# Two output-weight quarters stored as split halves and loaded again later; one V load and the kept stores queued behind the first Q copies

## The chip, the cores and the metric

One core of a Trainium2 chip runs the whole program. The metric is the device time of one execution in microseconds (us), the median over several runs. TensorE (PE in the profile) multiplies matrices, VectorE (DVE), ScalarE (ACT) and GpSimd (POOL) do the elementwise work, and SyncE (SP) issues most of the DMA transfers between the core's buffers and DRAM. ScalarE can issue transfers too, on a queue of its own.

## The reference

The input x has 2048 rows of 1024 float32. Two layers follow each other, then a last RMS normalisation:

```python
# layer A: chunked gMLP
u, v, z = split(rms_norm(x) @ w_in)                  # 3 x 2048 columns
v = layer_norm(gelu(v)); mixed = W_s (masked) applied over 128-row groups, per head
x = x + (gelu(u) * mixed * silu(z)) @ w_out
# layer B: band attention, 16 heads of 64
k, v = split(rms_norm(x, g_kv) @ w_kv)
q, z = split(rms_norm(x, b_g) @ w_qz)
o = softmax(q k^T / 8 + bias[rel]) v                 # own chunk of 64 rows and the 8 before
x = x + (o * silu(z)) @ wb_out                       # wb_out: 1024 x 1024
out = rms_norm(x, final_g)
```

Everything is float32, and so are the results.

## The kernel before

**Splitting.** Every float32 operand of a large product is split into a high half and a low half (a rounded copy by ScalarE, and the rest by a VectorE subtraction); a product is then three matmuls: high by high, high by low, low by high. The helper `mm3` does that (lines 111 to 113), and `split_in` (lines 241 and 242) splits a weight tile that has arrived as raw float32 in a buffer `raw_...`. Split weights lie in the tag "T", which has eight buffers of 512 KB; the raw ones in two buffers "wr" or four buffers "raw".

**Output product.** `o @ wb_out` is done in Strassen's way with seven products in place of eight, in the order `PHS = (1, 7, 2, 6, 5, 4, 3)`. Products 1, 2 and 3 need a plain quarter of `wb_out` (`o_raw = {1: (0, 0), 2: (1, 0), 3: (1, 1)}`); "quarter 2" below means the quarter of product 2, and so on. Products 4 to 7 need sums of quarters. Each quarter comes in two column parts, q = 0 and 1, and each part is 512 KB for the high half and 512 KB for the low half. The sums are formed once, in tile 1 (`o_sums`), split, and stored as halves in DRAM (`ows`); every later use loads two halves (line 294 or 1787). Quarters 1, 2 and 3 are loaded raw and split again at each use.

**Attention stage.** The 2048 rows are four tiles t of 512 rows. For each tile the kernel walks over eight pairs p of heads, and for each pair over eight steps u (two heads times four blocks of 128 queries). A step computes scores (`score`: matmuls at line 1541, bias and row minimum by VectorE at 1549, exponential by ScalarE at 1559, scaling by GpSimd at 1563), and turns the probabilities of two steps earlier (`flip`: TensorE transposes into `tp` at line 1579, ScalarE copy at 1583, VectorE subtraction at 1584). `value` multiplies by V (line 1604). Between these, TensorE is filled with projections for the next pair (`project`, `gate`: tiles `pj`) and with the output product of the tile before (`outs[t - 1]`), in shares fixed by the table `SHARE`. So products of tile 2 run within tile 3, and tile 3's own output product (`last_all`) begins in the last pair of tile 3 and ends the kernel. There `last_right` fetches the weights; for product 3 they go into the buffer of the transposed probabilities, for product 2 into the four raw buffers.

**Projections and Q.** `project` makes Q for one pair and copies each half to the other 64 partitions with a DMA (line 1482), four copies for a pair: a score needs both places. During the first pair (`held` is set) the stores of K and of the scaled projection weights are put on a list `kept` and issued by `keep_all()` after `values(0, 0)`, which loads V (line 1509).

**Order.** The program text gives a priority, and a planner orders each engine's and each queue's instructions by a simulated time; buffers are assigned in that order too. Where the text wants a fixed order it adds an edge without a semaphore: `follow(ins, names)` puts an instruction behind named ones, and `on_beat(ins)` puts it behind the latest transposes of `flip`. SP's queue issues strictly in order: an issue that waits for its data or its buffer holds all behind it.

Of the kernel before, what the change touches and what calls it, by code (L numbers as in the profile page):

```python
# [33 lines left out]
def trunk_kernel(  # L34
# [30 lines left out]
    }  # L65
    ows = {
        (ph, q): dram.tile([P, 2, 1024], F32, name=f"ows{ph}_{q}")
        for ph in range(4, 8) for q in range(2)
    }
    khd = [  # L70
        [dram.tile([2, P, T], F32, name=f"khd{t}_{p}") for p in range(NPAIR)]
# [134 lines left out]
    def on_beat(ins):  # L206
        if beat:
            tc.add_manual_dep(
                ins.ins, beat[-1],
                mybir.DependencyInfo(mybir.DependencyClass.NoSync, mybir.DependencyReason.DATA),  # L210
                reason="order",
            )
        return ins
# [31 lines left out]
    kept = []  # L245
    held = [0]

    def keep_all():
        while kept:
            nc.sync.dma_start(*kept.pop(0))  # L250

    early_w = {}

# [24 lines left out]
    def o_right(t):  # L278
        def right(ph):
            if (t, ph) in o_early:  # L280
                return o_early.pop((t, ph))
            out = []
            for q in range(2):
                name = f"bo{t}_{ph}_{q}"
                w = [w_tile(f"w{i}_{name}") for i in "hl"]
                if ph in o_raw:
                    raw = raw_w(1, f"raw_{name}")
                    nc.sync.dma_start(raw[:], wb_out[o_raw[ph]][q])
                    hi = split_in(raw, *w)
                    if (ph, q) == (1, 1):  # L290
                        on_beat(hi)
                else:
                    for i in range(2):
                        nc.sync.dma_start(w[i][:].bitcast(F32), ows[ph, q][:, i, :])
                out.append(w)
            return out
        return right
# [1135 lines left out]
    with ExitStack() as bctx:  # L1433
# [22 lines left out]
        def one(t, p, c):  # L1456
# [9 lines left out]
                    yield None  # L1466
            yield acc

        def project(t, p):
            for acc in one(t, p, 1):  # L1470
                yield
            for hd in range(2):
                qh = sb.tile([P, T], F32R, tag="Q", name=f"Qh{t}_{p}_{hd}", bufs=8)
                ql = sb.tile([P, T], F32R, tag="Q", name=f"Ql{t}_{p}_{hd}", bufs=8)
                r, r2 = halves(hd)
                nc.scalar.mul(qh[r, :], acc[r, :], 0.125)
                nc.vector.scalar_tensor_tensor(
                    ql[r, :], acc[r, :], 0.125, qh[r, :].bitcast(F32),
                    op0=ALU.mult, op1=ALU.subtract,
                )  # L1480
                for x_ in (qh, ql):
                    nc.sync.dma_start(x_[r2, :].bitcast(F32), x_[r, :].bitcast(F32))
                qt[t, p, hd] = (qh, ql)
            for acc in one(t, p, 0):
                yield
            for hd in range(2):
                r, r2 = halves(hd)
                kx = sb.tile([P, 2 * T], F32R, tag="K", name=f"K{t}_{p}_{hd}", bufs=4)
                nc.scalar.copy(kx[r, T:], acc[r, :])
                nc.vector.tensor_tensor(  # L1490
                    kx[r2, T:], acc[r, :], kx[r, T:].bitcast(F32), op=ALU.subtract
                )
                if t + 1 < NT:
                    k_store = (khd[t][p][hd], kx[:, T:].bitcast(F32))
                    if held:
                        kept.append(k_store)
                    else:
                        nc.sync.dma_start(*k_store)
                if t > 0:
                    nc.sync.dma_start(kx[:, :T].bitcast(F32), khd[t - 1][p][hd])  # L1500
                kt[t, p, hd] = kx
            if not held:
                keep_all()

        def values(t, p):
            v = vtl[t, p] = sb.tile([P, 8, 256], F32R, tag="V", name=f"V{t}_{p}", bufs=2)
            for i, tt in enumerate((t - 1, t)):
                if tt >= 0:
                    nc.sync.dma_start(v[:, i * TB : (i + 1) * TB, :].bitcast(F32), vhd[tt][:, p])

        def gate(t, p):
            for acc in one(t, p, 2):
# [142 lines left out]
            young.clear()  # L1655

        owed_out = []

        def send(dst, src):
            if la:  # L1660
# [4 lines left out]
        def send_all():  # L1665
            while owed_out:
                on_beat(nc.sync.dma_start(*owed_out.pop(0)))
# [96 lines left out]
        def last_right(ph, q):  # L1764
            name = f"bo_{ph}_{q}"
            if ph == 5:
                v = sb.tile([P, 8, 256], F32R, tag="V", name=f"w{name}", bufs=2)
                w = [v[:, i * 4 : i * 4 + 4, :].rearrange("p a b -> p (a b)") for i in range(2)]
            elif ph == 3:
                if q == 0:  # L1770
                    lw["pt"] = sb.tile([P, 5376], F32R, tag="PT", name=f"w{name}", bufs=1)
                w = [lw["pt"][:, (2 * q + i) * 1024 : (2 * q + i + 1) * 1024] for i in range(2)]
            elif ph == 2:
                w = [
                    sh.tile([P, 1024], F32R, tag="raw", name=f"w{i}{name}", bufs=4)[:]
                    for i in "hl"
                ]
            else:
                w = [w_tile(f"w{i}{name}")[:] for i in "hl"]
            if ph in o_raw:  # L1780
                raw = raw_w(NT - 1, f"raw_{name}")
                nc.sync.dma_start(raw[:], wb_out[o_raw[ph]][q])
                nc.scalar.copy(w[0], raw[:])
                tv(w[1], raw[:], w[0].bitcast(F32), op=sub)
            else:
                for i in range(2):
                    nc.sync.dma_start(w[i].bitcast(F32), ows[ph, q][:, i, :])
            lw[ph, q] = w
# [249 lines left out]
            score(0, 0, u)  # L2038
        held.clear()
        values(0, 0)  # L2040
        keep_all()
        before = None
        for t in range(NT):
            for p in range(NPAIR):
# [14 lines left out]
                for u in range(8):  # L2059
                    if u < 6:  # L2060
                        score(t, p, u + 2)
                    elif p + 1 < NPAIR or t + 1 < NT:
                        score(t + (p + 1) // NPAIR, (p + 1) % NPAIR, u - 6)
                    upto = total * (2 * u + 1) // per
                    take(gen, upto - done)
                    done = max(done, upto)
                    if u == 4:
                        value(t, p, 0)
                    elif u == 0 and before:
                        value(*before, 1)  # L2070
                    flip(t, p, u)
                    drain_all()
                    send_all()
                    square_all()
                    if u and finals:
                        finals.pop(0)()
                    if todo:
                        todo.pop(0)()
                    upto = total * (2 * u + 2) // per
                    take(gen, upto - done)  # L2080
                    done = max(done, upto)
# [64 lines left out]
```

## Time and profile before

| | |
|---|---|
| median of 3 runs | 2639.57 us (2638.92 to 2641.89) |
| profiled execution, its own time | 2640.17 us |
| its span | 2638.1 us |
| TensorE busy | 2604.5 us (99%) |
| VectorE, ScalarE, GpSimd busy | 71%, 50%, 34% |
| DMA, the SP queue | 704.25 MB, 78.1% of the 16 DMA engines |
| DMA in all | 720.31 MB, mean 273 GB/s |

The profile is of one execution. The span runs from its first to its last record; the profiled execution's own time is that of the device, 2.1 us more. Busy times are the union of the instructions of an engine. A wait "X <- Y" says that X's engine stood idle before X, and that Y ended that. A fence of times has the start in us, the duration in us, the engine, the line, the operation, output and inputs, and how many neighbouring instructions were merged; idle time ahead of it stands in brackets. SPq and ACTq are the issues of transfers on those engines' queues; their short durations are the issue alone, and the transfer lands later.

### The profile page before, as it was taken

How to read it: one execution, taken by the hardware profiler on the slowest of the kernel's cores; microseconds unless marked ns; L12 is line 12 of the kernel's file. 1: busy time of each engine (PE TensorE's matmuls, PEld its weight loads, DVE VectorE, ACT ScalarE, POOL GpSimd, SP SyncE). 2: the span in 40 equal slices, each digit the busy share in tenths (PEclk: the TensorE clock that was granted, in tenths of full speed). 3: DMA queues.
4: the chain of work that ended last, by engine and by line, in shares of the span. 5: the costliest groups of instructions: out<-in, count | busy, mean ns of one | idle time of the engine just before them, and what ended most of it. 6: DMA issues, size and time to landing. Idle time of an engine off the chain costs nothing. (4 is left out here: it accounts for less than half of the span.)

```text
span 2638.1 us, 38018 instructions
## 1 busy us (share of the span) xinstructions
PE 2604.5 (99%) x12976; PEld 2177.8 (83%) x12976; DVE 1871.4 (71%) x2942; ACT 1314.7 (50%) x2331; POOL 890.1 (34%) x871
## 2 busy tenths in 40 slices
PE   9999999999999999999999999999999999999997
PEld 7888888788888888888888878888888888888886
DVE  6655676766667668757776767778778777877677
ACT  6422243443433434343466466666656655666564
POOL 4611335143252332203334334343333322332245
PEclk9999999999999999999999999999999999999999
DMA  7898998999988968968886587778787767775676
GB/s 299 316 345 332 347 364 319 315 327 328 333 302 303 331 224 310 342 205 262 322 279 234 184 277 236 233 244 260 248 278 253 228 208 222 252 228 162 192 229 249
DMA packets 275153, 720.31 MB, mean 273 GB/s; under 512 B 28944, under 2 KB 68880, under 8 KB 274960
## 3 DMA queue, kind: packets, MB, share of 16 engines
q1 hardware_dynamic: 268096, 704.25, 78.1%
q10 hardware_dynamic: 6864, 13.63, 1.4%
q8 instruction: 104, 1.70, 0.3%
q14 instruction: 89, 0.73, 0.1%
HBM read 532.69 MB, written 174.59 MB: 268 GB/s over the span
## 5 line engine op out<-in xcount | busy, mean ns | idle before, releaser
L111 PE MATMUL P<-T,S 128*128 128x512 f32 x1248 | 495.3, 397 | 0.0
L113 PE MATMUL P<-T,S 128*128 128x512 f32 x1248 | 487.6, 391 | 0.1
L112 PE MATMUL P<-T,S 128*128 128x512 f32 x1248 | 487.0, 390 | 0.0
L1563 POOL TENSOR_SCALAR pr<-pr,sl 128x640 f32<-128x640 f32 (+4 forms) x256 | 207.9, 812 | 554.1 <-DVE sl L1562 477.7
L111 PE MATMUL pj<-hh_b,wh_b 128*128 128x512 f32 x768 | 318.6, 415 | 0.0
L113 PE MATMUL pj<-hh_b,wl_b 128*128 128x512 f32 x768 | 304.0, 396 | 0.3 <-DVE wl_b L242 0.2
L112 PE MATMUL pj<-hl_b,wh_b 128*128 128x512 f32 x768 | 302.7, 394 | 0.0
L1559 ACT ACTIVATE pr<-pr,nm 128x640 f32<-128x640 f32 (+4 forms) x256 | 195.6, 764 | 198.8 <-DVE nm L1549 196.6
L113 PEld LDWEIGHTS P<-T,S 128*128 128x128 f32 x1248 | 234.3, 188 | 51.0 <-DVE S L463 0.4
L112 PEld LDWEIGHTS P<-T,S 128*128 128x128 f32 x1248 | 235.0, 188 | 44.7 <-DVE T L463 0.4
L111 PEld LDWEIGHTS P<-T,S 128*128 128x128 f32 x1248 | 234.7, 188 | 44.5 <-issue 0.2
L1584 DVE TENSOR_TENSOR pt<-tp,pt 128x640 fp32r<-128x640 f32 (+4 forms) x256 | 188.7, 737 | 48.9 <-ACT pt L1583 46.0
L1549 DVE CUSTOM_DVE_ANT_0 pr<-s,bias 128x640 f32<-128x640 f32 (+4 forms) x256 | 188.3, 736 | 43.8 <-PE s L1541 38.8
L1583 ACT CAST pt<-tp 128x640 fp32r<-128x640 f32 (+4 forms) x256 | 158.6, 619 | 38.5 <-PE tp L1579 32.6
L1579 PE MATMUL tp<-ident,pr 128*128 128x128 f32 x1120 | 166.5, 274 | 8.5 <-DVE pt L1584 7.4
L113 PEld LDWEIGHTS pj<-hh_b,wl_b 128*128 128x128 f32 x768 | 144.2, 188 | 34.5 <-DVE wl_b L242 2.3
L1579 PEld LDWEIGHTS tp<-ident,pr 128*128 128x128 f32 x1120 | 130.9, 140 | 42.5 <-issue 13.8
L111 PEld LDWEIGHTS pj<-hh_b,wh_b 128*128 128x128 f32 x768 | 145.1, 189 | 17.7 <-ACT wh_b L241 1.2
L1604 PEld LDWEIGHTS pv<-pt,V 128*128 128x128 f32 x896 | 142.8, 188 | 20.3 <-DVE pt L1584 3.4
L112 PEld LDWEIGHTS pj<-hl_b,wh_b 128*128 128x128 f32 x768 | 145.1, 189 | 16.5
L1604 PE MATMUL pv<-pt,V 128*128 128x256 f32 (+3 forms) x896 | 154.8, 320 | 0.8 <-ACT pt L1583 0.5
L242 DVE TENSOR_TENSOR wl_b<-raw_b,wh_b 128x1024 fp32r<-128x1024 f32 x96 | 121.0, 1261 | 25.1 <-ACT wh_b L241 22.9
(307 smaller groups left out, 5720.8 us busy)
## 6 DMA issues: line engine op xcount, KB each, us to landing
S<-hsd SPq DMA_DIRECT2D x288, 512.0 KB, 5.3
rw<-in_w_a SPq DMA_DIRECT2D x108, 512.0 KB, 6.2
raw_b<-wk SPq DMA_DIRECT2D x75, 512.0 KB, 4.5
A<-ytd SPq DMA_DIRECT2D x72, 512.0 KB, 5.7
hsd<-S SPq DMA_DIRECT2D x56, 512.0 KB, 4.9
V<-vhd SPq DMA_DIRECT2D x56, 512.0 KB, 5.6
bias<-reld SPq DMA_DIRECT2D x64, 320.0 KB, 4.0
va<-vd SPq DMA_DIRECT2D x32, 512.0 KB, 5.7
```

Source lines behind the costliest of these rows:

```text
L111: first = mm(ps, lh, rh, start=first, stop=False)
L112: mm(ps, lh, rl, start=False, stop=False)
L113: mm(ps, ll, rh, start=False, stop=last)
L242: tv(wl[:], raw[:], wh[:].bitcast(F32), op=sub)
L1549: peak = nc.vector.tensor_tensor_reduce(out=pr[:, c0:].rearrange("p (a b) -> p a b", a=nseg), in0=ps[:, :nseg, :w], in1=bias[:, c0:].rearr ...
L1559: nc.scalar.activation(pr[:, c0:], pr[:, c0:], AF.Exp, scale=-1.0, bias=nm[:], accum_out=sl[:])
L1563: nc.gpsimd.tensor_scalar(pr[:, c0:], pr[:, c0:], sl[:], 1.0, op0=ALU.mult, op1=ALU.mult)
L1579: ins = tpose(tp[:, b, :], pr[:, b * P : (b + 1) * P], ident[:])
L1583: nc.scalar.copy(oh, tp[:, b0:5, :].rearrange("p a b -> p (a b)"))
L1584: nc.vector.tensor_tensor(pt[:, 2560 + o + b0 * P : 2560 + o + 640], tp[:, b0:5, :].rearrange("p a b -> p (a b)"), oh.bitcast(F32), op=ALU ...
L1604: mm(po[:, q0 * P : q1 * P], vtl[t, p][:, i, hs], rhs, start=(i == blocks[0] and j == 0), stop=(i == 7 and j == 1),)
```

## The change

Part one concerns the output weights. `ows` gets entries for products 2 and 3 too. When tile 1's product 3 and tile 2's product 2 have split their raw quarters, the four halves of each are put on a list `halves_out`, and at each later step u, after `flip` and its followers, one of them is stored by ScalarE's queue. Tile 2's product 3 and the last tile's products 2 and 3 then load halves and do not split. Quarter 1 is split at every use as before, and so are quarter 2 in tiles 0 to 2 and quarter 3 in tiles 0 and 1.

Part two concerns the first pair of the attention stage. The names of its four Q copies are collected in `twins`; the V loads of tile 0 and the kept stores that are issued after `values(0, 0)` get an edge that puts them behind those copies on SP's queue.

```diff
     ows = {
         (ph, q): dram.tile([P, 2, 1024], F32, name=f"ows{ph}_{q}")
-        for ph in range(4, 8) for q in range(2)
+        for ph in range(2, 8) for q in range(2)
     }
...
-    def keep_all():
+    def keep_all(names=()):
         while kept:
-            nc.sync.dma_start(*kept.pop(0))
+            follow(nc.sync.dma_start(*kept.pop(0)), names)
...
-                if ph in o_raw:
+                if ph in o_raw and (t, ph) != (2, 3):
                     raw = raw_w(1, f"raw_{name}")
                     nc.sync.dma_start(raw[:], wb_out[o_raw[ph]][q])
                     hi = split_in(raw, *w)
                     if (ph, q) == (1, 1):
                         on_beat(hi)
+                    if (t, ph) in ((1, 3), (2, 2)):
+                        halves_out.extend(
+                            (ows[ph, q][:, i, :], w[i][:].bitcast(F32)) for i in range(2)
+                        )
                 else:
...
+        twins = []
...
                 for x_ in (qh, ql):
-                    nc.sync.dma_start(x_[r2, :].bitcast(F32), x_[r, :].bitcast(F32))
+                    ins = nc.sync.dma_start(x_[r2, :].bitcast(F32), x_[r, :].bitcast(F32))
+                    if not t + p:
+                        twins.append(ins.ins.name)
...
-                    nc.sync.dma_start(v[:, i * TB : (i + 1) * TB, :].bitcast(F32), vhd[tt][:, p])
+                    ins = nc.sync.dma_start(
+                        v[:, i * TB : (i + 1) * TB, :].bitcast(F32), vhd[tt][:, p]
+                    )
+                    if not t:
+                        follow(ins, twins)
...
+        halves_out = []
...
-            if ph in o_raw:
+            if ph == 1:
                 raw = raw_w(NT - 1, f"raw_{name}")
...
-        keep_all()
+        keep_all(twins)
...
                     send_all()
+                    if halves_out:
+                        on_beat(nc.scalar.dma_start(*halves_out.pop(0)))
                     square_all()
```

## The prediction

> **What bounds the kernel now.** I read the page first: busy time by engine, then the busy time in stretches of the span, then TensorE's own waits, and last the engines' timelines at the two places that the diff touches.
>
> ```profile
> span 2638.1 us, 38018 instructions
> ...
> PE 2604.5 (99%) x12976; PEld 2177.8 (83%) x12976; DVE 1871.4 (71%) x2942; ACT 1314.7 (50%) x2331; POOL 890.1 (34%) x871
> ```
>
> TensorE is busy for all but 33.6 us of the span, and the change neither adds nor removes a matmul. So nothing can be won except out of those 33.6 us, and only where they lie beside the change. The next view gives busy time by stretch; the number after each stretch's length is TensorE's.
>
> ```profile
> core 0: us, PE busy (x) PEld busy (x) DVE busy (x) ACT busy (x) POOL busy (x), PEclk, DMA share, GB/s
> 1515.00:1545.00 30.00, 28.38 (x130) 21.98 (x128) 19.24 (x43) 17.80 (x35) 5.05 (x9) 1.00 0.94 304
> 2200.00:2300.00 100.00, 99.17 (x547) 85.15 (x545) 77.41 (x140) 63.06 (x115) 31.31 (x40) 1.00 0.75 241
> ...
> 2560.00:2580.00 20.00, 17.20 (x91) 13.43 (x91) 19.15 (x32) 14.02 (x28) 9.49 (x8) 1.00 0.83 283
> 2580.00:2605.00 25.00, 22.34 (x118) 18.32 (x117) 19.36 (x36) 12.75 (x24) 11.89 (x13) 1.00 0.96 329
> ...
> 2629.00:2638.00 9.00, 0.00 (x0) 0.00 (x0) 5.28 (x11) 0.81 (x3) 1.10 (x2) 0.63 0.49 183
> ```
>
> The reader is to see where TensorE stands idle: 1.62 us where the first pair of the attention stage starts, 0.83 us at the border of tiles 2 and 3, 2.80 and 2.66 us in the last pair of the last tile, where VectorE is busy 19.15 of 20 us, and 9 us of tail without a matmul. TensorE's waits over the whole span say for what:
>
> ```profile
> engine line waited for: us in total, times, longest us
> PE tp L1579 <- DVE pt L1584: 7.4, 14, 1.1
> PE s L1541 <- DMA Qh<-Qh: 1.4, 1, 1.4
> PE bo L112 <- DVE wbo L1784: 1.3, 2, 0.7
> ```
>
> The second row is the first pair's Q copy, the third the split of quarter 3 in the last output product; the first is VectorE's half of the transposed probabilities, of which the change can reach the share that lies in the last pair.
>
> **Edit 1: V loads and kept stores behind the Q copies.** Nothing is removed; on SP's queue the first V load, two kept stores of projection weights and two of K go behind the four Q copies of the first pair.
>
> ```profile
> 1521.45 1.03 SPq L1509 DMA_DIRECT2D V<-vhd  x1
> 1522.57 1.31 SPq L1482 DMA_DIRECT2D Qh<-Qh  x1
> ...
> 1530.87 0.44 SPq L263 DMA_DIRECT2D raw_b<-in_w_kqz  x1
> ```
>
> ```profile
> 1522.57 8.08 DMA Qh<-Qh
> ```
>
> ```profile
> 1530.79 0.30 PE L1541 MATMUL s<-K,Qh 128*128 128x128 f32 x1 [1.42 <-DMA Qh<-Qh]
> ...
> 1544.19 0.51 PE L1604 MATMUL pv<-pt,V 128*128 128x512 f32 x1
> ```
>
> The third fence shows the score that waited 1.42 us for this copy, the second that the copy took 8.08 us from issue to landing. The V load issued just ahead of it is 512 KB, an estimated 1.7 us at the 304 GB/s of this stretch, and its own issue took 1.03 us. Without it the copy goes out 1.0 us and lands 2.7 us earlier; the score needs 1.42. Bounds: 0 (if the copy is slow for another reason) and -1.42 (the whole wait); I take -1.4, as 2.7 is nearly twice the need; a loss is excluded as long as the two covers that follow hold. What moves behind: the V load comes about 4 us later (four copies of about 1 us issue each), near 1525.5, and is needed at 1544.19; with the 8.08 us that a transfer can take here it still has 10 us. The kept weight stores hold a raw buffer that the load at 1530.87 refills; those weights reach TensorE only after GpSimd's scaling:
>
> ```profile
> 1548.54 1.90 POOL L226 TENSOR_TENSOR raw_b<-raw_b,kg 128x1024 f32<-128x1024 f32 x1
> ```
>
> That is 17.7 us after the load, so a 5 us delay costs 0. Without that cover each microsecond beyond it would be one on TensorE.
>
> **Edit 2: halves stored once, loaded later.** Removed: the splits of quarter 3 for tile 2's output product, and of quarters 2 and 3 in the last product, two column halves each, so six ScalarE copies and six VectorE subtractions. Durations:
>
> ```profile
> L241 ACT CAST wh_bo<-raw_bo x18: 1042/1052/1058, 1864.8 to 2556.5; 128x1024 fp32r<-128x1024 f32 x18
> L242 DVE TENSOR_TENSOR wl_bo<-raw_bo,wh_bo x18: 1204/1226/2322, 1869.0 to 2559.3; 128x1024 fp32r<-128x1024 f32 x18
> L1784 DVE TENSOR_TENSOR wlbo<-raw_bo,whbo x4: 1209/1214/2085, 2568.8 to 2593.9; 128x1024 fp32r<-128x1024 f32 x4
> L1784 DVE TENSOR_TENSOR wbo<-raw_bo,wbo x2: 1710/2010/2309, 2620.8 to 2622.5; 128x1024 fp32r<-128x1024 f32 x2
> ```
>
> Two of the 18 go, two of the next four (quarter 1 stays split), and both of the last: about 6 x 1.05 = 6.3 us of ScalarE. Where the VectorE ones stand:
>
> ```profile
> 2555.62 2.32 DVE L242 TENSOR_TENSOR wl_bo<-raw_bo,wh_bo 128x1024 fp32r<-128x1024 f32 x1
> 2559.26 1.68 DVE L242 TENSOR_TENSOR wl_bo<-raw_bo,wh_bo 128x1024 fp32r<-128x1024 f32 x1
> 2581.65 1.21 DVE L1784 TENSOR_TENSOR wlbo<-raw_bo,whbo 128x1024 fp32r<-128x1024 f32 x1
> ...
> 2620.84 3.94 DVE L1784 TENSOR_TENSOR wbo<-raw_bo,wbo 128x1024 fp32r<-128x1024 f32 x2
> ...
> 2630.58 0.68 DVE L1957 TENSOR_TENSOR row<-bo,ou 128x512 f32<-128x512 f32 x1
> ```
>
> ```profile
> 2564.96 0.74 PE L1579 MATMUL tp<-ident,pr 128*128 128x128 f32 x5 [0.41 <-DVE pt L1584]
> 2567.57 0.56 PE L1541 MATMUL s<-K,Qh 128*128 128x320 f32 x2 [0.49 <-DVE nm L1549]
> 2577.90 0.50 PE L1604 MATMUL pv<-pt,V 128*128 128x512 f32 x1 [0.46 <-ACT pt L1583]
> 2586.04 0.74 PE L1579 MATMUL tp<-ident,pr 128*128 128x128 f32 x5 [1.08 <-DVE pt L1584]
> ...
> 2588.70 0.40 PE L112 MATMUL bo<-wlbo,Qho 128*128 128x512 f32 x1
> ...
> 2628.60 0.39 PE L113 MATMUL bo<-wbo,Qlo 128*128 128x512 f32 x1
> ```
>
> Last pair: the subtractions of 2.32 and 1.68 us (quarter 3 of tile 2's product) go from in front of the waits of 0.41 and 0.49 us, which are both smaller than what goes. The wait of 0.46 us is for a ScalarE copy of probabilities that stood right behind a copy of quarter 2,
>
> ```profile
> 2576.21 1.05 ACT L1783 CAST whbo<-raw_bo 128x1024 fp32r<-128x1024 f32 x1 [2.49 <-DMA raw_bo<-in_wb_out]
> ```
>
> and that goes too. The 1.21 us goes from in front of the 1.08 us, of which I count a half, since VectorE has other work without a gap there. Together 0.41 + 0.49 + 0.46 + 0.54 = 1.9 us. The rest of the idle time of these stretches follows quarter 1's splits and the output scalings, which stay. Bounds: 0 (a loss here could only come from the loads, priced below) and the whole 2.80 + 2.66 = 5.46; I take 1.9, also because what is late next is close, the loaded halves of Strassen product 7:
>
> ```profile
> 2578.46 0.40 SPq L1787 DMA_DIRECT2D wlbo<-ows  x1
> ```
>
> ```profile
> DMA to landing us min/median/max: 6.0/8.2/10.6
> ```
>
> Issued at 2578.46, with the median of 8.2 us for such halves it lands at 2586.7, and TensorE takes it up at 2588.70: 2.0 us of slack, which a gain of 1.9 uses up.
>
> End: the 1.3 us wait for the split of quarter 3 goes wholly if its halves have landed; bounds 0 and -1.3, taken -1.3, for it is the last product and its loads need no engine any more. VectorE's last addition starts at 2630.58, 1.59 us after the last matmul's end (2628.60 + 0.39), because the 3.94 us put VectorE behind. Bounds for the tail 0 and -1.6; the scalings of the other rows still stand there, so -1.0. End together: -2.3.
>
> Added: eight stores of 512 KB on ScalarE's queue, four near the border of tiles 2 and 3 and four in tile 3; twelve loads of halves in place of six raw loads; 14 x 0.524 = 7.3 MB more in all. A store's issue on that queue, in this trace:
>
> ```profile
> 1495.88 0.38 ACTq L1425 DMA_DIRECT2D vhd<-v  x1
> ```
>
> Eight make 3 us of issuing, with ScalarE busy half its time (50%): 0, if the half is ready when its store comes up; the rival with ScalarE held has the price if not. A store reads its weight buffer for up to four steps, about as long as the product itself, so it delays no refill; if it did, the nearest row is the 0.83 us of idle at that border, which could double. Quarter 3's loads for tile 2 now wait on SP for a weight buffer, where before ScalarE's copy waited; behind them on SP stand the bias loads for the next scores and the stores of the output. The six extra loads meet a DMA share of 0.83 to 0.96 in the last pair, an estimated 1.6 us each at 329 GB/s. Bounds for all added transfers 0 and 6 x 1.6 = 9.6; nearest is the share of 0.83, which still has gaps, so most are free, and I take half of one, +0.8.
>
> **Sum.** -1.4 - 1.9 - 2.3 + 0.8 = -4.8 us against the profiled execution's 2640.17, which is 0.6 above the median of the three runs. From the median 2639.57 this gives 2634.8, or -0.18%. A measurement of this kernel tells about 0.2% from no change, here 5.3 us, so the forecast stands just inside that bound.
>
> **Rivals.** *Nearly the whole idle goes.* VectorE, once ahead, takes the waits behind quarter 1's splits with it: 5.0 instead of 1.9 in the last pair. For it: VectorE is the only engine near its limit there (19.15 of 20 us). Against: product 7's halves with their 2.0 us. -7.9, so 2631.7.
>
> *The loads take the gain.* The four halves of quarter 2 can be loaded as soon as their buffers are free, ahead of product 7's; three more 512 KB transfers there are 4.8 us against 2.0 us of slack, so +2.8 on TensorE: -4.8 + 2.8 = -2.0, so 2637.6. For it: the share of 0.96. Against: the gaps that a share of 0.83 leaves before.
>
> *The stores delay the tile border.* Four stores of 512 KB at 241 GB/s are 2.2 us each; if SP's loads behind them come later by that and TensorE pays all of it, +8.7: 2643.5. Against: a share of 0.75 there. The Trainium skill ("DMA: Bandwidth & Descriptors", section "Issuing engines are not separate DMA queues") says that DMAs of all issuing engines run on the same 16 DMA engines and interleave, so that ScalarE's queue would give the stores no bandwidth of their own; by that rule taken to its end the sum is this rival's +3.9, by the row of the share it is the forecast's -4.8. No run shown yet has stores beside loads at this place.
>
> *ScalarE is held: slower.* A store of a low half waits, at the head of ScalarE's queue, for VectorE's subtraction, and the softmax copies queue behind it.
>
> ```profile
> 2552.19 1.06 ACT L241 CAST wh_bo<-raw_bo 128x1024 fp32r<-128x1024 f32 x1
> ```
>
> This copy ends at 2553.24 and its subtraction at 2557.94, 4.7 us later. Four low halves (two quarters, two column halves) held 4.7 us each are 18.8 us: 2639.57 + 18.8 - 4.8 = 2653.6 if TensorE pays all. It decides from 2.5 us each: 10.1 us are needed to turn -4.8 into +5.3. Against: one store goes out per step, after that step's transposes, so mostly later than its subtraction.
>
> *Edit 1 does nothing*, the copy being slow behind still earlier transfers: 1.4 less, 2636.2.
>
> **Chances.** Forecast 0.43 (its own range 2632.8 to 2636.8, that is 2 us to each side, about the spread between 1.9 and 5.46 less what product 7 holds back), nearly the whole idle 0.20, loads take the gain 0.19, edit 1 idle 0.06, border 0.05, ScalarE held 0.07. Faster than 2634.3 is the second case and 0.18 of the first: 0.38. Slower than 2644.8 is the held case: 0.07. The rest is 0.55. The range runs from 2631.0, which keeps most of the second case, to 2640.0, which keeps the loads and leaves out border and held case.
>
> **What would show it.** Right: the first score no longer waits for Qh; copies into wh_bo are x16 and none goes into wbo; the last product runs without a wait and its last addition follows the last matmul closely; the last pair has under 4 us of idle. Wrong: ScalarE idle until a subtraction before a store; TensorE waiting for DMAs into whbo or wlbo; new waits at the tile border, or on the splits of the projection weights, where SP's order shifted.

## The result, and the profile after

The changed kernel takes 2635.59 us in the median against 2638.96 us for the kernel before, measured beside each other; the ratio is 0.9982, 95% interval [0.9976, 0.9988]. That is -0.18%, 4.75 us, the size that the prediction gave (-4.8 us). How large the gain is, is less certain than this agreement suggests: the interval runs from 3.2 to 6.3 us, and the medians themselves are 3.4 us apart, the means 4.4. A second measurement on another chip gave 2636.02 against 2639.38 us, ratio 0.9985 [0.9977, 0.9994]. That the kernel became faster is clear; since the range of the prediction reached up to 2640.0 us, a result inside it says little by itself. The total came out as forecast, but its terms did not: two gains were larger, and one forecast gain was a loss.

The page of the profiled execution, span and busy time by engine:

```profile
span 2634.2 us, 38034 instructions
...
PE 2605.1 (99%) x12976; PEld 2178.3 (83%) x12976; DVE 1857.8 (71%) x2936; ACT 1310.4 (50%) x2325; POOL 888.4 (34%) x871
```

The span is 3.9 us shorter than the one profiled before; TensorE's busy time is the same within 0.6 us, so what was won was idle time. TensorE's waits over the whole span (engine, line, what it waited for, us in total, times, longest):

```profile
PE tp L1591 <- DVE pt L1596: 5.2, 11, 1.1
...
PE s L1553 <- DVE nm L1561: 1.8, 1, 1.8
```

The rows of before for the Q copy (1.4 us) and for the split of quarter 3 (1.3 us) are gone. The wait for the transposed probabilities fell from 7.4 to 5.2 us. One row has grown: a score waits 1.8 us for a row minimum, where the longest such wait before was 0.5 us. TensorE's timeline at the three places that the change touches (start, duration, instruction; in brackets the idle time ahead of it and what ended it):

```profile
1529.62 0.39 PE L112 MATMUL pj<-hl_b,wh_b 128*128 128x512 f32 x1
1530.12 0.30 PE L1553 MATMUL s<-K,Qh 128*128 128x128 f32 x1
```

```profile
2572.91 0.74 PE L1591 MATMUL tp<-ident,pr 128*128 128x128 f32 x5 [0.56 <-DVE pt L1596]
...
2577.57 0.56 PE L1553 MATMUL s<-K,Qh 128*128 128x320 f32 x2 [1.82 <-DVE nm L1561]
...
2587.70 0.74 PE L1591 MATMUL tp<-ident,pr 128*128 128x128 f32 x5 [1.13 <-DVE pt L1596]
```

```profile
2623.99 0.39 PE L113 MATMUL bo<-wbo,Qlo 128*128 128x512 f32 x1
```

The first score starts 0.50 us behind the last projection matmul in front of it, where it was 1.81 us (1528.98 to 1530.79). The score still starts right behind the landing of its Q copy, 0.13 us later, as before: the copy, issued at 1522.05, takes 7.94 us (before: 8.08), but counted from the last projection matmul it goes out 1.2 us earlier. In the last pair three waits of 0.2 us and more are left, where before had nine. The longest of them stands behind a scaling on VectorE:

```profile
2573.19 2.98 DVE L1920 SCALAR_TENSOR_TENSOR y<-y,rr_f,gf 128x512 f32<-128x512 f32 x2 [0.43 <-POOL rr_f L126]
2576.09 0.68 DVE L1970 TENSOR_TENSOR ou<-bo,ou 128x512 f32<-128x512 f32 x1
2576.70 0.81 DVE L1561 CUSTOM_DVE_ANT_0 pr<-s,bias 128x640 f32<-128x640 f32 x1
```

The third row makes the row minimum. The last product runs without a wait. How much each place gave is read from the starts of the same matmuls, counted in TensorE's order, in both traces:

| stretch | before | after |
| --- | --- | --- |
| last projection matmul to first score | 1.81 | 0.50 |
| last pair: a transpose near 2555 to a matmul of the last tile's output near 2598, 205 matmuls later | 2554.83 to 2599.52: 44.69 | 2555.38 to 2596.78: 41.40 |
| from there to the start of the last matmul | 29.09 | 27.20 |
| end of the last matmul to the end of the span | 9.14 | 9.81 |

So -1.3, -3.3, -1.9 and +0.7 us, together -5.8; another +0.5 us comes from the projection of tile 3 (below). The remaining difference to the spans' -3.9 us, +1.4 us, lies in two stretches in which executions differ anyway: the first 1517 us (+0.6; between 1511.1 and 1518.4 us in the thirteen profiles of this study) and the border of tiles 1 and 2 (+0.7; between 94.0 and 96.3 us).

The table's third row is longer than TensorE's wait there. Here are the matmuls of the last product before, around one of its two waits:

```profile
2621.53 0.39 PE L111 MATMUL bo<-wbo,Qho 128*128 128x512 f32 x1
2622.60 0.50 PE L112 MATMUL bo<-wbo,Qho 128*128 128x512 f32 x1 [0.69 <-DVE wbo L1784]
2622.94 0.39 PE L113 MATMUL bo<-wbo,Qlo 128*128 128x512 f32 x1
```

The wait in brackets is 0.69 us. But matmuls of this shape follow each other every 0.23 us, and the one behind the wait starts 1.07 us after its forerunner, and the next one again 0.34 us later: the wait cost 0.84 + 0.11 = 0.95 us. A duration of 0.39 us overlaps the next matmul's, so the idle time in brackets starts only 0.16 us after the moment at which TensorE could have gone on. Ahead of a group of transposes only these 0.16 us come on top: the group that waited 0.91 us in the last pair before started at 2570.92, 1.30 us behind its forerunner, and the matmul behind it followed after 0.49 us, where it follows a group without a wait after 0.46 to 0.48 us.

The tail, on VectorE (additions L1970, scalings L1920):

```profile
2623.17 1.42 DVE L1920 SCALAR_TENSOR_TENSOR row<-row,rr_f,gf 128x512 f32<-128x512 f32 x2 [0.66 <-POOL rr_f L126]
2624.50 1.28 DVE L1970 TENSOR_TENSOR row<-bo,ou 128x512 f32<-128x512 f32 x2
...
2629.38 1.42 DVE L1920 SCALAR_TENSOR_TENSOR row<-row,rr_f,gf 128x512 f32<-128x512 f32 x2 [0.66 <-POOL rr_f L126]
```

The last matmul ends at 2624.38. The last two additions come together at 2624.50, behind the scaling of another row block; then two row blocks go through square, root and scaling one after the other. Before, the scaling of row block 3 also stood in front of the last addition, but only that one addition was left; the one of the product's first half had run ahead of it:

```profile
2627.58 0.69 DVE L1957 TENSOR_TENSOR row<-bo,ou 128x512 f32<-128x512 f32 x1
...
2628.99 1.41 DVE L1907 SCALAR_TENSOR_TENSOR row<-row,rr_f,gf 128x512 f32<-128x512 f32 x2 [0.66 <-POOL rr_f L126]
```

TensorE's order has changed there too. Before, the last product's two column halves ran one after the other, and the first was complete at 2626.26; in the changed kernel the planner mixes them, to be seen where two matmuls of line 111 follow each other, and both become complete close to the end:

```profile
2620.81 0.62 PE L111 MATMUL bo<-wbo,Qho 128*128 128x512 f32 x2
```

### The profile page after: what moved, and what is told of

It reads as the page before. It is cut to its first block, busy times and chain, and to the rows that moved or that the text cites. A ratio compares the mean times of both kernels' runs of the same rounds, so it can differ in the third digit from the quotient of the medians.

```text
span 2634.2 us, 38034 instructions
## 1 busy us (share of the span) xinstructions
PE 2605.1 (99%) x12976; PEld 2178.3 (83%) x12976; DVE 1857.8 (71%) x2936; ACT 1310.4 (50%) x2325; POOL 888.4 (34%) x871
```

## The experiments

Every ratio is against the kernel before on the same chip. "Last pair", "last product" and "tail" are the last three rows of the table, read in the same way.

**Each part alone.** First the reordering of SP's queue without the halves; against the changed kernel:

```diff
-        for ph in range(2, 8) for q in range(2)
+        for ph in range(4, 8) for q in range(2)
...
-                if ph in o_raw and (t, ph) != (2, 3):
+                if ph in o_raw:
...
-            if ph == 1:                      # last_right
+            if ph in o_raw:
```

`halves_out` is gone with them.

> Only the first part of the change: the first tile's V loads and kept stores behind the first pair's Q copies; the output-weight quarters as in the kernel before. My theory: the 1.3 us between the last projection matmul and the first score go (1.81 us before, 0.50 us in the changed kernel), little else moves: about 1.1 to 1.3 us less than before, a ratio near 0.9995. The last pair and the end as before: about 6 us of TensorE idle between 2534 and 2603, a wait of 1.3 us at the last product. Rival (what comes first now delays the next transfers, so that a later wait takes the gain back): first score early by 1.3 us, but nothing left at the border of the first two tiles; ratio 1.000. Rival (the gain at the first score was a shift between two executions): the first score waits as before.

Ratio 0.9997 [0.9988, 1.0005]: by this measurement alone, no difference from before. In its trace the first score follows after 0.58 us (1530.71 to 1531.29), and it still waits 0.19 us for the copy. Last pair 44.68 us, last product 29.07, tail 9.17, as before. Over all profiles the gap is 1.81 and 1.46 us in the two kernels without this part and 0.22 to 0.69 us in ten executions with it, but 1.19 us in the second profile of the changed kernel: the gain is about 1.2 us, with single executions that keep half of it. In all thirteen profiles the copy takes 7.5 to 8.6 us, with and without the V load ahead of it, so the gain is its earlier issue and no faster transfer. Then the halves alone:

```diff
-        keep_all(twins)
+        keep_all()
...
-                    if not t:
-                        follow(ins, twins)
```

> Only the second part of the change: the halves stored and loaded; SP's queue at the first pair as before. My theory: the first score waits 1.3 us longer than in the changed kernel, the last pair loses 3.2 us of idle time against before and the last product's wait of 1.3 us is gone, the tail behind the last matmul is 9.8 us as in the changed kernel (9.1 before): 3.3 to 3.8 us less than before, ratio near 0.9986. Rival (the two parts help each other, the transfers of the first tile set the stores or the weights behind): less than the difference of the changed kernel and the first part alone, under 2.5 us, ratio 0.9991 or more.

Ratio 0.9988 [0.9980, 0.9997], near the theory's 0.9986, though the interval also holds the rival's 0.9991; last pair 41.57, last product 27.20, tail 9.57 us, and 1.46 us to the first score. By these stretches the two parts add up; the ratios alone could not show it.

**The halves, user by user.** Only product 3 of the tile before the last loads halves:

```diff
-            if ph == 1:                      # last_right
+            if ph in o_raw:
...
-                    if (t, ph) in ((1, 3), (2, 2)):
+                    if (t, ph) == (1, 3):
```

> The changed kernel, but the halves are stored for quarter 3 alone and loaded only by product 3 of the tile before the last; both products of the last tile split raw quarters again. Theory (each subtraction that VectorE loses shortens the waits behind it): the two subtractions of 2.32 and 1.68 us in front of the waits of 0.41 and 0.49 us before are gone, so that 1 to 2 us of the 3.2 us of the last pair are kept; the last product waits 1.3 us for its splits as before, the tail is 9.1 us as before. With 1.2 us of the first part: 2.2 to 3.2 us less than before, ratio 0.9988 to 0.9992. Rival (the gain in the last pair comes from quarter 2's split on ScalarE and VectorE or from the transfers that move, not from these two subtractions): less than 0.5 us in the last pair, ratio 0.9994 to 0.9996.

Ratio 0.9989 [0.9981, 0.9998]. Last pair 42.11 us, so 2.6 of the 3.3 us come from this one user; last product 28.87, tail 9.38 us. TensorE's waits in the last pair:

```profile
2569.93 0.74 PE L1591 MATMUL tp<-ident,pr 128*128 128x128 f32 x5 [0.22 <-DVE pt L1596]
...
2574.51 0.56 PE L1553 MATMUL s<-K,Qh 128*128 128x320 f32 x2 [1.75 <-DVE nm L1561]
...
2581.76 0.74 PE L1591 MATMUL tp<-ident,pr 128*128 128x128 f32 x5 [1.10 <-DVE pt L1596]
```

Six waits of before (0.24, 0.41, 0.49, 0.91, 0.53, 0.46 us) are replaced by 0.22 and 1.75 us. So the two splits of this user had held all six, not only the two waits behind them, and the time that they free ends at a new wait. That VectorE's subtractions did it, and not ScalarE's copies, is likely by where they stand on VectorE, but not shown. The wait of 0.46 us, which the prediction put down to a copy of quarter 2 on ScalarE, is gone although that copy stays here. The wait of 1.1 us is untouched. With the last product alone on halves:

```diff
-            if ph == 1:                      # last_right
+            if ph in (1, 2):
...
-                if ph in o_raw and (t, ph) != (2, 3):
+                if ph in o_raw:
```

> The changed kernel, but the halves are stored for quarter 3 alone and loaded only by the last tile's last product; product 3 of the tile before and product 2 of the last tile split raw quarters. Theory: the last product's wait of 1.3 us goes whole and the matmuls behind 2603 end 1.3 to 1.9 us earlier; the tail behind the last matmul grows to 9.6 to 9.9 us (from 9.1), since the addition of the last product's first half stays behind a scaling of 1.42 us; the last pair as before within 0.8 us. With 1.2 us of the first part: 1.8 to 2.6 us less than before, ratio 0.9990 to 0.9993. Rival (the tail grew in the changed kernel because quarter 2's split was gone as well, which let the scalings of the rows come earlier): tail 9.1 us or less here, 3 us less than before, ratio 0.9988.

Ratio 0.9994 [0.9985, 1.0002]. The last product takes 27.22 us: the whole 1.9 us come from its own halves. But the tail takes 11.30 us, neither value expected, and gives 2.2 us back. VectorE behind the last matmul, which ends at 2624.62:

```profile
2627.68 1.41 DVE L1920 SCALAR_TENSOR_TENSOR row<-row,rr_f,gf 128x512 f32<-128x512 f32 x2 [0.67 <-POOL rr_f L126]
2629.01 0.68 DVE L1970 TENSOR_TENSOR row<-bo,ou 128x512 f32<-128x512 f32 x1
```

The addition of the last product's second half, whose matmul was done at 2624.62, runs at 2629.01, behind two scalings and a root. TensorE's order at the end is that of before, without its waits; what costs 2 us is the order on VectorE.

**VectorE's subtraction kept.** As many bytes and transfers as in the changed kernel, ScalarE's copies away, but VectorE still subtracts (the same edit in `last_right`):

```diff
+                elif ph == 3:
+                    nc.sync.dma_start(w[0][:].bitcast(F32), ows[ph, q][:, 0, :])
+                    raw = raw_w(1, f"raw_{name}")
+                    nc.sync.dma_start(raw[:], wb_out[o_raw[ph]][q])
+                    tv(w[1][:], raw[:], w[0][:].bitcast(F32), op=sub)
```

> The changed kernel, but for quarters 2 and 3 of the last tile and for product 3 of the tile before it the low half is not loaded: the raw quarter is loaded in its place (as many bytes, as many transfers) and VectorE subtracts the loaded high half from it. ScalarE's copies stay away. Theory (what VectorE no longer subtracts is the gain): the subtractions of 1.2 to 2.3 us each come back ahead of TensorE's waits, the last pair loses at most 1 us of idle time against before instead of 3.2, the last product waits again for about 1.3 us; with the first part's 1.2 us the time is 1.2 to 2.7 us below before, ratio 0.9990 to 0.9995. Rival (the gain of the last pair comes from the loads that moved forward, the raw quarter of product 1 by 20 to 35 us above all, and from ScalarE's copies): the last pair as in the changed kernel, ratio 0.9982 to 0.9985.

Ratio 1.0014 [1.0005, 1.0023]: slower than before, which neither theory expected. In the last pair the waits of 0.2 us and more sum to 4.4 us (5.7 before, 3.5 after), in between the two theories; this does not tell how much of that gain belongs to the subtractions and how much to ScalarE's copies. The loss is in the last product, 33.99 us (counted by the number of the matmul; TensorE's order differs a little in this kernel), where TensorE also waits 0.29 and 1.28 us for copies by ScalarE:

```profile
2624.95 1.28 DVE L1980 TENSOR_TENSOR row<-bo,ou 128x512 f32<-128x512 f32 x2
2626.42 0.16 DVE L1912 TENSOR_TENSOR rr_f<-ssq 128x1 f32<-128x1 f32 x1 [0.19 <-ACT jk L1892]
2626.50 1.23 DVE L1807 TENSOR_TENSOR wbo<-raw_bo,wbo 128x1024 fp32r<-128x1024 f32 x1
```

```profile
2627.78 0.80 PE L112 MATMUL bo<-wbo,Qho 128*128 128x512 f32 x1 [3.16 <-DVE rr_f L125]
2628.37 0.63 PE L113 MATMUL bo<-wbo,Qlo 128*128 128x512 f32 x1
```

The raw quarter was issued at 2608.88 and took 10.7 us, so it lay there at 2619.5; but the subtraction stands in VectorE's queue behind the addition and the root sum of a row block, and starts at 2626.50. TensorE stood for 3.16 us, and its next matmuls took 0.63 us instead of 0.39, at a granted clock of 0.50 for 3.4 us.

**The price of the stores.** Nothing loads the halves here, so all users split raw quarters; each half is stored twice, 16 stores instead of 8:

```diff
-                            (ows[ph, q][:, i, :], w[i][:].bitcast(F32)) for i in range(2)
+                            (ows[n, q][:, i, :], w[i][:].bitcast(F32))
+                            for i in range(2) for n in (ph, ph + 6)
...
-                    if halves_out:
+                    for _ in range(2 if halves_out else 0):
```

> The changed kernel with the first part as it is, but nothing loads the halves: all users split raw quarters as in the kernel before, and each half is stored twice from ScalarE's queue, to two places, so 16 stores of 512 KB in place of 8. Theory (a store costs ScalarE's queue 0.33 us of issue and the transfers have room, DMA share 0.75 before between 2200 and 2300): the stretch from 2240 to 2440 us is as long as before within 0.4 us, everything else as with the first part alone; 1.2 us less than before or as it is, ratio 0.9995 to 1.0000. Rival (stores hold ScalarE or the DMA engines so that each costs time): 16 stores at 0.33 us on the path are 5.3 us more, ratio 1.0015; at half of it 2.6 us more, ratio 1.0006.

Ratio 1.0029 [1.0017, 1.0041], 7.8 us slower in the median, more than even the rival asked for. But it is no price per store: by the starts of the same matmuls, 9.2 us against before arise between 2200 and 2300, near 2275 us, and 2.0 us between 2400 and 2500. SP's queue near 2275, then GpSimd:

```profile
2263.63 1.00 SPq L1861 DMA_DIRECT2D or<-x1d  x1
2273.38 0.32 SPq L1677 DMA_DIRECT2D x2d<-ou  x1
```

```profile
2272.05 1.30 POOL L1973 TENSOR_TENSOR ou<-ou,or 128x512 f32<-128x512 f32 x1 [3.75 <-DMA or<-x1d]
...
2278.54 0.15 POOL L1273 MEMSET bias<- 64x64 f32 x1 [4.40 <-DMA bias<-reld]
```

A load of the residual (or) is issued at 2263.63, in a stretch where the DMA share is 1.02 (2260 to 2270; 0.95 in the changed kernel). It takes 8.3 us (such loads 6.2 and 6.8 us before, 5.1 and 5.2 us in the changed kernel, between 2240 and 2300). GpSimd waits 3.75 us for it, until 2272.05; the store of GpSimd's result (x2d) holds SP's queue until 2273.38; the bias load behind it goes out only then, and GpSimd waits 4.40 us for that. This chain alone is not the cause: in the next run, with eight stores, GpSimd waits 3.88 us for the residual and the same store holds SP's queue until 2274.20, and TensorE loses no time. What differs is when the data comes. Counted from the same matmuls (this execution was 6.8 us ahead of before at 2200), the bias lands when it did before, but the residual 5.4 us and the next tile's rows 4.7 us later; their transfers were 1.5 and 1.7 us slower, and the rest is later issue. The splits of these rows, and scalings, then stand on VectorE ahead of row minima that TensorE waits for:

```profile
2276.85 0.56 PE L1554 MATMUL s<-K,Qh 128*128 128x320 f32 x2 [1.59 <-DVE nm L1562]
```

The planner has also given this kernel another order: at 84 of the 2942 places in VectorE's order and 28 of the 1756 in SP's stands another instruction than with eight stores. How much of the loss comes from the sixteen transfers and how much from that order was not separated. TensorE by stretches of 2 us (length, busy time of PE, PEld, DVE, ACT, POOL with counts, granted clock, DMA share, GB/s):

```profile
2276.00:2278.00 2.00, 0.85 (x4) 0.59 (x4) 2.00 (x5) 2.00 (x5) 0.00 (x0) 1.00 0.99 232
2278.00:2280.00 2.00, 0.85 (x4) 0.59 (x4) 2.00 (x5) 2.00 (x5) 1.31 (x3) 1.00 0.93 341
2280.00:2282.00 2.00, 1.18 (x5) 0.81 (x5) 1.81 (x3) 0.55 (x2) 0.56 (x2) 0.72 1.02 412
2282.00:2284.00 2.00, 1.03 (x3) 1.03 (x4) 1.92 (x4) 2.00 (x4) 0.78 (x1) 0.50 1.10 385
```

TensorE is idle for 4.8 of the 10 us from 2274 to 2284. Its granted clock falls behind 2280 and is 0.50 until 2287.7; with 0.72, 0.50, 0.50 and 0.57 in four stretches of 2 us that costs another 3.4 us. With eight stores and no loads from them (the last hunk undone, and `range(2)` over `ph` alone as in the changed kernel):

> The changed kernel with the first part as it is, but nothing loads the halves: the eight stores of 512 KB are made once, all users split raw quarters as in the kernel before. Theory (the eight stores have room, the sixteen had not: one load of the residual landed late behind them and held SP's queue, and the idle time of TensorE that followed lowered its clock): no idle time over 1.5 us and a granted clock of 1.00 between 2200 and 2300 us; as long as with the first part alone, ratio 0.9995 to 1.0000. Rival (each store costs, and eight cost half of sixteen, 4 to 5 us, which the changed kernel's loads win back elsewhere): ratio 1.0010 to 1.0015.

Ratio 1.0000 [0.9991, 1.0008], which cannot be told from the first part alone. The trace has no such place, and its granted clock stays at 1.00 (the same columns):

```profile
2200.00:2300.00 100.00, 99.10 (x539) 84.37 (x538) 79.44 (x141) 63.11 (x114) 30.73 (x41) 1.00 0.81 264
```

TensorE is idle for 0.90 of 100 us, before 0.83. So eight stores cost nothing that can be measured here. One small price was found: in all kernels that store quarter 2's halves once in tile 3 the stretch from 2417 to 2555 takes 138.2 to 138.3 us instead of 137.8 to 137.9 (139.9 with sixteen stores). No wait is listed in it: in two places the planner now puts two projection matmuls more ahead of a group of transposes, and the group starts 0.4 us behind its forerunner instead of 0.2 us.

**The tail by hand.** The last product's two column halves one after the other on TensorE, and on VectorE each late addition ahead of a scaling:

```diff
+                    if i == 13:                       # last_all
+                        follow(ins, [ahead_])
...
-                    tv(o, ps, y, op=add)              # evict
+                    added = tv(o, ps, y, op=add)
+                    while last and late:
+                        late.pop(0)([added.ins.name])
...
+                if last and b in (0, 3):              # finish
+                    late.append(scale)                # scale follows the names given
```

> The changed kernel with the order of the end written out: the last product's two column halves one after the other on TensorE, not mixed; on VectorE the scaling of row block 3 behind the addition of the first half, that of row block 0 behind the addition of the second. Theory (the order of VectorE's queue sets the tail, 1.42 us of scaling in front of each late addition): the addition behind the last matmul starts within 0.2 us of its end instead of 0.8 us later with two additions in a row, and the last scaling ends 1.6 to 2.2 us earlier; tail behind the last matmul 7.6 to 8.2 us instead of 9.81, ratio 0.9974 to 0.9976 against before. Rival (the output's last stores and their landing set the end, or the squares and roots do): tail within 0.5 us of the changed kernel's, ratio 0.9980 to 0.9983.

Ratio 0.9975 [0.9966, 0.9984], tail 8.16 us instead of 9.81:

```profile
2626.15 0.68 DVE L1977 TENSOR_TENSOR row<-bo,ou 128x512 f32<-128x512 f32 x1
2626.89 1.41 DVE L1924 SCALAR_TENSOR_TENSOR row<-row,rr_f,gf 128x512 f32<-128x512 f32 x2
```

No matmul or transfer was taken away; only the order on two engines. The tail shows the gain; the ratio alone does not separate this kernel from the changed one, whose interval was 0.9976 to 0.9988. TensorE's order at the end is now that of before and of the run with 11.30 us, so between these two it is the order on VectorE that makes 3.1 us. In the next run, two more edits: the second half of row block 0's scaling behind the root of row block 2, and the first scaling of the tile before (two instructions, 2.98 us, in front of the row minimum of the new wait) dealt out over two steps:

```diff
+                elif t + 2 == NT and b == 1:          # finish
+                    then = finals[:1]
+                    finals[:1] = [lambda: scale(halves=(0,)),
+                                  lambda: (scale(halves=(1,)), *(f() for f in then))]
...
+                    while half:                       # finish, row block 2
+                        half.pop(0)([rooted.ins.name])
```

> The changed kernel with the order of the end written out as in the run before that did so, and two edits more: the second half of row block 0's scaling stands behind the root of row block 2, and the first row block's scaling of the tile before (two instructions of 1.5 us together in front of a row minimum) is dealt out over two steps. Theory: the last scaling starts 0.5 us earlier (it stood behind two scalings, now behind one and a half), and TensorE's wait of 1.8 us for the row minimum shrinks by 0.7 to 1.8 us: 1.0 to 2.0 us less than with the tail's order alone, ratio 0.9968 to 0.9971 against before. Rival (the waits of the last pair stand behind VectorE's whole queue, so a scaling that moves only moves the wait): the row minimum's wait goes and comes back at a later step, ratio 0.9973 to 0.9976.

Ratio 0.9976 [0.9964, 0.9987], no better. The row minimum's wait fell from 1.82 to 1.30 us and the last pair to 40.68 us (41.89 with the tail's order alone, 41.40 in the changed kernel), but the tail grew to 8.59 us:

```profile
2626.60 0.55 POOL L126 TENSOR_TENSOR rr_f<-rr_f,mhalf 128x1 f32<-128x1 f32 x1 [1.78 <-DVE rr_f L125]
2628.40 0.98 POOL L126 TENSOR_TENSOR rr_f<-rr_f,mhalf 128x1 f32<-128x1 f32 x1 [1.25 <-DVE rr_f L125]
```

GpSimd's root took 0.98 us instead of 0.55 where a scaling of VectorE now ran beside it. Without the cut, that is without the second hunk, beside the changed kernel again:

> The changed kernel with the order of the end written out and the first row block's scaling of the tile before dealt out over two steps, but without the last scaling cut apart (there GpSimd's root took 0.98 us beside VectorE in place of 0.55 us, and the tail came out at 8.6 in place of 8.2 us). Theory: tail 8.0 to 8.3 us, idle time of TensorE in the last pair 2.5 to 3.2 us (3.5 us in the changed kernel): 2.0 to 2.6 us less than the changed kernel, ratio 0.9970 to 0.9975 against before. Rival (the last pair's waits follow VectorE's whole queue and only move): last pair 3.5 us or more, ratio as with the tail's order alone.

> The changed kernel as it is, on the chip of the two others, for a direct comparison: ratio 0.9980 to 0.9985 against before; tail behind the last matmul 9.8 us, idle time in the last pair 3.5 us.

Ratio 0.9975 [0.9967, 0.9984], 2633.09 us, beside 2636.02 us and 0.9985 [0.9977, 0.9994] for the changed kernel on that chip. The intervals overlap, so that 3 us are likely but not certain. Idle time in the last pair 3.1 us, as forecast. In the changed kernel's second profile it was not the expected 3.5 but 2.0 us: the wait of 1.13 us is absent, and of the large ones only the one for the row minimum, 1.78 us, is left. All the same the last pair took 41.17 us there (40.99 here), because the granted clock was 0.50 for 3.4 us behind that wait. Tail 8.84 us (9.71): the tail missed its 8.0 to 8.3 us, since the last matmul had moved up to 2622.17 and the last addition, at 2623.11, stood behind a scaling again. Splitting the scaling brought no gain in the total that can be seen.

## Why the prediction was right, point by point

- **First score, -1.4.** Shown: 1.3 us in the profile, 1.2 us in the part alone, though the second profile of the changed kernel kept a gap of 1.19 us. Half of the step was wrong: the copy goes out earlier, but without the V load ahead of it it is no faster (7.94 us, before 8.08), so the 1.7 us of transfer were not saved, and there was no reserve of "nearly twice the need". The earlier issue alone just sufficed, which was luck. The rival by which this part does nothing falls by the gaps, not by the ratio. Neither cover failed: no wait for V or for kg's weights appears at that place.
- **Last pair, -1.9.** Mis-sized: -3.3. The removed splits, with subtractions of 2.32 and 1.68 us, did hold the waits of 0.41 and 0.49, but four more waits went with them, the 0.46 us among them, which the prediction had put down to quarter 2. The 1.21 us of quarter 2 in front of the 1.08 us, counted at half, gave nothing in the first profile, where 1.13 us is still there, and is gone in the second; this term stays open. What was late next was not product 7's halves but the row minimum, 1.82 us, behind the output scaling that the prediction had named as staying. And every wait was priced by its bracket, which is 0.16 to 0.27 us too little.
- **Last product, -1.3.** Direction right, size 1.9, for that same reason: two waits of 0.69 and 0.57 us cost 1.89.
- **Tail, -1.0.** The step that failed: +0.7. It took VectorE's lateness from 3.94 us of splits, and let the end come forward as far as the last addition. That addition did move up, from 1.59 to 0.73 us behind the last matmul's end. But what stands behind it, to the end of the last scaling, grew from 4.5 to 5.7 us: before, the addition of the product's first half had run earlier, so that its row block's root ran beside the last addition; now both additions come together, and VectorE stands idle for 1.6 us behind them, waiting for a square and two roots, where it was 0.7 us for one root. Two orders make that, the mixed halves on TensorE and the scaling ahead of both additions on VectorE. The runs do not separate these two; with unmixed halves the tail was 8.16 or 11.30 us, by VectorE's order.
- **Transfers, +0.8.** About +0.5, and not from transfers: no wait for a DMA into `whbo`, `wlbo` or `wbo` shows up, and the half microsecond is the order of two groups of matmuls, which is there with the stores alone too.
- **The rivals.** "Nearly the whole idle goes" was half right in the last pair (3.3 of the 5.0), and the tail took some of it back. "The loads take the gain": quarter 2's first half was loaded already at 2460.0, far ahead, and nothing waited. "ScalarE is held" did not occur: stores were issued in 0.33 us each. "The stores delay the tile border" did not occur at eight stores. At sixteen, time was lost at that place and SP's loads came later, as it named, but with another order of the engines too. The Trainium skill's rule quoted beside that rival ("DMA: Bandwidth & Descriptors", section "Issuing engines are not separate DMA queues"), that DMAs of all queues share the same engines, is not contradicted: two loads on SP's queue took 8.3 and 8.5 us there, 6.8 us each before. But beside eight stores they took 5.2 to 7.2 us, so the rule alone does not tell when a store costs time.

That the total came out so close was luck: a tail that was wrong by 1.7 us and a last pair and product that were too small by 2.0 us cancelled. The mechanism, less VectorE work ahead of TensorE's waits, was right for the last pair and the last product.

## What to carry to other kernels

Price a wait by the distance between the starts of the instructions around it, not by the idle time in brackets: here 0.16 to 0.27 us more each, about a third of the gain in the last pair and the last product. When work is taken from an engine that runs in order, follow its queue beyond the first wait: here six waits went, up to a scaling that itself waited for GpSimd in the first profile. At a program's end look for what stands in the last engine's queue between the last matmul and the last store: writing out that order was worth 1.65 us of tail, about as much as the removal of the last product's splits. And compare the engines' orders whenever a planner makes them: in this case an edit of a few transfers also moved matmuls and scalings.

## What the runs showed of the hardware

TensorE's clock fell without a long pause. In the run with sixteen stores no idle time ahead of a matmul near 2275 was longer than 1.59 us; four of 1.0 to 1.6 us stand within 8 us, and the granted clock was 0.50 from 2280.9 to 2287.7, where matmuls took 0.63 us instead of 0.39. One wait can be enough, but need not be. In the changed kernel's second profile the wait of 1.78 us for the row minimum was followed by a granted clock of 0.50 for 3.4 us; in its first profile the same wait, 1.82 us, left it at 1.00. The same 15 matmuls behind that wait, in the first and in the second profile:

```profile
2578.49 2.46 PE L1616 MATMUL pv<-pt,V 128*128 128x512 f32 x15
```

```profile
2576.84 3.87 PE L1616 MATMUL pv<-pt,V 128*128 128x512 f32 x15
```

In the run with the subtraction kept the clock fell during the wait of 3.16 us. The Trainium skill ("TensorE: Matmul & The Clock Gate", section "Why this matters for your kernels") advises against idle gaps over about 3 us. That last case agrees; the others show that shorter gaps can do the same. What decides it was not found out. The price is on record: half the clock for 6.8 us near 2280 cost 3.4 us, for 3.4 us in the second profile 1.7 us.
